# Transformer block with two feed-forward layers: sums of down weight blocks on VectorE, another order of the seven block products, norms of the first rows given row by row

## Chip, cores and metric

The kernel runs on one core of one Trainium2 chip. The metric is device time in microseconds of one execution. A profiled execution gives a trace; its span runs from the first instruction to the last. In the profile PE is TensorE (PEld its weight loads), DVE is VectorE, ACT is ScalarE, POOL is GpSimd, and SP is the engine whose queue issues the DMAs.

## What is computed

One encoder layer on x of 1024 tokens by 1024 features, float32:

```python
f = swiglu(rmsnorm(x, ffn1_pre_g), ffn1_w_gate, ffn1_w_up, ffn1_w_down)   # silu(h @ Wg) * (h @ Wu) @ Wd
x = x + 0.5 * rmsnorm(f, ffn1_post_g)
h = rmsnorm(x, mix_pre_g);  qkv = h @ w_qkv
x = x + rmsnorm(concat(attention_a(qkv), attention_b(qkv)) @ w_out, mix_post_g)
f = swiglu(rmsnorm(x, ffn2_pre_g), ffn2_w_gate, ffn2_w_up, ffn2_w_down)
x = x + 0.5 * rmsnorm(f, ffn2_post_g)
```

The hidden width of the feed-forwards is 2816 = 22 x 128. The change touches the down projection h @ Wd of both feed-forwards and the norm behind it; attention is as it was.

## The kernel before, in words

Products of float32 are made of three passes: each operand is split into a high part, rounded by ScalarE (L118), and a low part, the rest (L119, on VectorE or GpSimd); high by high, high by low and low by high are added in PSUM.

The down projection is done as a seven-product block scheme. Tokens are halved (y rows T = 0 to 3 and 4 to 7), output columns are halved (0 to 511, 512 to 1023), and the hidden rows are taken in 11 pairs of two blocks of 128. For pair j the weight blocks b11, b12 (rows of the first block) and b21, b22 (of the second) are 128x512 each. Seven products k = 0 to 6 of a left factor (a sum of blocks of the hidden activations, kept in DRAM as hd) and a right factor take the place of eight. The right factors are, in turn: 0: b11; 1: b21; 3: d = b22 - b12; 2: s = b11 + d; 4: b21 - s; 5: b22 - s; 6: b22. `prepare_down` (L247 to L269) makes them in place: on GpSimd d in b12 (L261) and s in b11 (L262) at product 0, b21 - s in b12 (L264) and b22 - s in b11 (L265) at product 3.

The pairs are worked in two groups, of 5 and of 6 pairs, and each group goes through the seven products in the order DOWN = 0, 2, 3, 4, 5, 1, 6; within a product over the pairs. One item is one product of one pair: `down` (L343) issues 12 matmuls, three passes into each of four PSUM banks (i = 0 to 3). Products 0 and 1 add up in four banks of the pool psd, the others in the banks pa to pd of the pools psg0 and psg1; a product in `first` starts its banks new, the others go on adding. When the last pair of a product is done its four banks are read: product 0 into U by ScalarE (L369), product 2 is added to U (L371), the others go to the quarters of y with or without U (L378, L380, L382). In the second group U is added to three quarters of y by twelve delayed adds (L374), kept in the list `late`.

`run` (L441) goes through the items. Before each, `feed` (L201) prepares tiles of split factors until five (WBUFS) are ahead of TensorE; an item of the down projection uses two, one of each factor. Then one delayed job is taken from `late`: besides the twelve adds these are the last sums of left factors, each with its store to hd (L336, L337). After some items of the last two products of the second group (n - at = 0 for the first item of product 1, 6 for the first of product 6) `run` calls jobs: `begin1` loads gains and residuals; `post1((4, 5))` norms two finished rows of y at once, `rms_pair` (L96) giving both factors and `post_scale` (L526) doing both rows (L534, L535) with one store each; `mix1` (L628) is the norm ahead of the attention projection; `early1` and `early2` do squares and the gain product (L552, on GpSimd) of the first 512 columns of rows 0 to 3; `first_q` splits the first projection weight (L582, L583); `to_actT` (L111) turns a row on TensorE (L107) through psd. The last item does products of the last two pairs bank by bank, and `row1` or `row2` finishes each of rows 0 to 3.

Each engine works off its instructions in the order of its queue. The framework sets this order from the source order and the dependences, so that a queue can take a later instruction first (a store of the last pair's left factor, L330, is issued at 455.89 us, before the loop reaches the end of that pair). A load that takes a buffer over waits in the SP queue for its last reader. Of each weight block there are 6 buffers. b11 of the first five pairs is loaded when the gate and up products end (L430), in the space that the raw gate weights leave; b22, b12 and b21 at product 0; those of the second group one block per product, at products 4, 5, 1 and 6 of the first group (L269).

Of the kernel before, what the change touches and what calls it, by code (L numbers as in the profile page):

```python
# [20 lines left out]
D = 1024  # L21
# [15 lines left out]
def tile_macaron_block(ctx, tc, x, f1_pre, f1_post, f1_g, f1_u, f1_d, mix_pre, mix_post, w_qkv,  # L37
# [83 lines left out]
    class Ffn:  # L121
# [10 lines left out]
        PAIRS = NF // 2  # L132
        DOWN = (0, 2, 3, 4, 5, 1, 6)
        GROUPS = (tuple(range(PAIRS // 2)), tuple(range(PAIRS // 2, PAIRS)))
# [5 lines left out]
        def __init__(self, wg, wu, wd, tag, far):  # L140
            self.wg, self.wu, self.wd, self.tag, self.far = wg[0], wu[0], wd[0], tag, far
            self.near = "left" if far == "right" else "right"
            self.W, self.RAW, self.H, self.P, self.B, self.Q = {}, {}, {}, {}, {}, {}
            self.A, self.S = {}, {}
            self.items = [("G", i, p) for i in range(1, NF) for p in (self.ORDER if i < NF - 1 else self.LAST)]
            downs = [("D", k, j) for g in self.GROUPS for k in self.DOWN for j in g]
            self.items += downs
            self.tiles = []
            for it in self.items:
                self.tiles += [it] if it[0] == "G" else [it + (z,) for z in range(2)]  # L150
            self.wanted = [d[1:] for d in downs]
            self.hd = {}
            for key in self.wanted:
                self.hd[key] = dram.tile([128, 512], F32, name=f"hd{tag}" + "_".join(str(z) for z in key))
            self.made = self.used = 0
            self.dw = {}
            self.late = []

# [88 lines left out]
        def prepare_down(self, k, j, part):  # L247

            sub, add, tt = OP.subtract, OP.add, POOL.tensor_tensor
            if part == 0:  # L250
                self.load_left(1)
                self.split_w((j, k, 0), self.A.pop((k, j)), DVE)
                return
            n = len(self.GROUPS[0])
            if k == 0 and j < n:
                for b in ("b22", "b12", "b21"):
                    self.load_block(j, b)
            b11, b12, b21, b22 = [self.B[j, name] for name in self.BLOCKS]
            self.split_w((j, k, 1), (b11, b21, b11, b12, b12, b11, b22)[k], DVE)
            if k == 0:  # L260
                tt(b12, b22, b12, op=sub)  # L261
                tt(b11, b12, b11, op=add)  # L262
            elif k == 3:
                tt(b12, b21, b11, op=sub)  # L264
                tt(b11, b22, b11, op=sub)  # L265
            elif k in (1, 4, 5, 6) and j < n:
                for after in ((n,) if j == 0 else ()) + (j + n + 1,):
                    if after < self.PAIRS:
                        self.load_block(after, {4: "b12", 5: "b11", 1: "b21", 6: "b22"}[k])  # L269

# [72 lines left out]
        def down(self, k, js, y, ps, psd, row=None):  # L343
            g = js[0] in self.GROUPS[1]
            start, end = js[0] == self.GROUPS[g][0], js[-1] == self.GROUPS[g][-1]
            first = k in (0, 2, 3, 5)
            U, add, tt = self.U, OP.add, DVE.tensor_tensor
            Q = self.Q.setdefault(k < 2, {})
            for i in range(4):
                if first and start:  # L350
                    if k == 0:
                        Q[i] = psd.tile([128, 512], F32, name="pd")
                    else:
                        Q[i] = ps[i // 2].tile([128, 4, 128], F32, name="p" + "abcd"[i]).rearrange("p t f -> p (t f)")
# [9 lines left out]

                def yv(T, d):
                    return y[:, T, 512 * d:512 * d + 512]

                if k == 0:
                    ACT.activation(U[i], p, AF.Copy)  # L369
                elif k == 2:  # L370
                    tt(U[i], U[i], p, op=add)  # L371
                    if g:
                        for v in (yv(i + 4, 1), yv(i + 4, 0), yv(i, 1)):
                            self.late.append(lambda v=v, i=i: tt(v, v, U[i], op=add))  # L374
                else:
                    v = {1: yv(i, 0), 3: yv(i + 4, 1), 4: yv(i + 4, 0), 5: yv(i + 4, 1), 6: yv(i, 1)}[k]
                    if g or k == 5:
                        tt(v, v, p, op=add)  # L378
                    elif k == 1:
                        ACT.activation(v, p, AF.Copy)  # L380
                    else:
                        tt(v, U[i], p, op=add)  # L382
                if row:
# [7 lines left out]
        def gate_up(self, i, prod, ps, y, psd):  # L391
# [32 lines left out]
            if i == NF - 1 and n == 3:  # L424
                self.close_tx(3)
                self.raw.release()
                self.load_left(self.AHEAD)
                self.open_blocks(("b11", "b12"), self.far)
                self.open_blocks(("b22", "b21"), self.near)
                for j in self.GROUPS[0]:  # L430
                    self.load_block(j, "b11")
            if n == 6 and i % 2 == 1:
# [8 lines left out]
        def run(self, ps, y, psd, jobs, row):  # L441
# [4 lines left out]
            for n, it in enumerate(self.items):  # L446
                if n == at:
                    self.add_late(len(self.late))
                    for name in ("b12", "b11"):
                        self.dw[name].release()  # L450
                self.feed()
                self.add_late(1)
                if it[0] == "G":
# [69 lines left out]
    def junk(T):  # L523
        return actT[:, HI, :, T]
# [20 lines left out]
    def post_early(T, g):  # L545

        if T % 2 == 0:
# [3 lines left out]
                       accum_out=SS[T // 2][:, 0, T % 2:T % 2 + 1])  # L551
        POOL.tensor_tensor(yh, yh, g[:, 0:512], op=OP.mult)  # L552

# [67 lines left out]

    def post1(Ts):
        r = rms_pair([y[:, T, :] for T in Ts], [junk(T - 4) for T in Ts])
        post_scale(Ts, r, E1["g"], [E1["xr", T] for T in Ts], lambda T: x1d[T])
        for T in TS[TS.index(Ts[0]) + 2:TS.index(Ts[0]) + 4]:
            E1["xr", T] = load_res(E1["pre"], lambda T: xrow(xv, T), T, 2)

# [9 lines left out]
    def early1():  # L637
        for T in range(4):
            post_early(T, E1["g"])

    def row1(i):
        post_late(i)
        if i % 2 == 1:
# [4 lines left out]

    f1.run((psg0, psg1), y, psd,
           {0: [begin1, lambda: post1((4, 5))], 3: [lambda: mix1((4, 5))], 4: [lambda: post1((6, 7))],  # L650
            5: [early1], 6: [lambda: mix1((6, 7))], 7: [first_q], 8: [lambda: to_actT(4, y[:, 4, :], psd)],
            9: [lambda: to_actT(5, y[:, 5, :], psd)]}, row1)
    psg1.release()
# [7 lines left out]

    def turn1(T):
        to_actT(T, y[:, T, :], psd)

    mix1((0, 1))
# [431 lines left out]

    def post2(Ts):
        r = rms_pair([y[:, T, :] for T in Ts], [junk(T - 4) for T in Ts])
        post_scale(Ts, r, E2["g"], [E2["xr", T] for T in Ts], lambda T: xrow(ov, T))  # L1100

# [7 lines left out]

    f2.run((psg0, psg1), y, psd, {0: [begin2, lambda: post2((4, 5))], 4: [lambda: post2((6, 7))], 5: [early2]}, row2)  # L1110
    psg1.release()
# [71 lines left out]
```

## Time and profile before

| | us |
|---|---|
| median of 3 runs | 2070.18 |
| lowest and highest | 2069.85, 2072.19 |
| the profiled execution | 2066.44 |
| its span | 2064.7 |
| TensorE busy in the span | 1986.9 |
| VectorE, ScalarE, GpSimd busy | 1353.2, 1030.1, 995.4 |
| mean granted clock of TensorE | 0.992 |

The down projection of the first feed-forward lies from 473.84 to 717.04 us, that of the second from 1817.28 to 2052.00. A matmul's busy time overlaps with the next one's, so stretches are compared by their length from first start to next start. Idle time in a row of the timeline stands in brackets, with the instruction that ended it.

### The profile page before, as it was taken

The page shows a single profiled execution, that of the slowest core. Times are in us where ns is not written, and L with a number is a line of the kernel's source. Part 1 is how long each engine was busy: PE and PEld are TensorE (multiplying, and loading weights), DVE is VectorE, ACT ScalarE, POOL GpSimd, SP SyncE. Part 2 cuts the span into 40 slices and gives each one's busy share as a digit, 9 for nine tenths or more (in the row PEclk, how much of TensorE's full clock was granted, in tenths as well). Part 3 has the DMA queues.
Part 4 walks back from the last instruction along what each step waited for, and adds up shares of the span by engine and source line. Part 5 has one row for each costly group of instructions (what it writes and reads, how often), then busy time and mean ns, then how long its engine had stood idle before and what let it go on. Part 6 is the DMA issues. An engine that isn't in the chain of part 4 may idle for free. (4 is left out here: it accounts for less than half of the span.)

```text
span 2064.7 us, 30519 instructions
## 1 busy us (share of the span) xinstructions
PE 1986.9 (96%) x10704; PEld 1676.6 (81%) x10704; DVE 1353.2 (66%) x2323; ACT 1030.1 (50%) x1977; POOL 995.4 (48%) x864
## 2 busy tenths in 40 slices
PE   7999999999998899999999999999999999999986
PEld 6777777777776799998999998887777777777775
DVE  7555454558667948766988887365555545586678
ACT  5433333334443844546999998234333333344434
POOL 4566656655142102124777887315566566651421
PEclk9999999999999999999999999999999999999998
DMA  4233332327533462232040752322323324275333
GB/s 148 72 103 98 107 102 82 123 92 260 174 113 93 165 182 89 76 92 60 1 138 18 201 137 82 104 74 72 102 87 118 103 77 128 84 268 174 112 104 152
DMA packets 212440, 235.62 MB, mean 114 GB/s; under 512 B 22208, under 2 KB 148160, under 8 KB 212160
## 3 DMA queue, kind: packets, MB, share of 16 engines
q1 hardware_dynamic: 212288, 233.69, 36.3%
q8 instruction: 84, 1.38, 0.3%
q14 instruction: 68, 0.56, 0.1%
HBM read 166.01 MB, written 67.63 MB: 113 GB/s over the span
## 5 line engine op out<-in xcount | busy, mean ns | idle before, releaser
L119 POOL TENSOR_TENSOR wgu<-rawgu,wgu 128x512 fp32r<-128x512 f32 x216 | 313.4, 1460 | 362.1 <-ACT wgu L118 334.7
L118 ACT ACTIVATE wgu<-rawgu 128x512 fp32r<-128x512 f32 x302 | 181.7, 628 | 378.0 <-POOL rawgu L227 189.8
L286 PE MATMUL pa<-actT,wgu 128*128 128x512 f32 (+1 forms) x1080 | 270.5, 398 | 8.9 <-ACT U L405 8.1
L286 PEld LDWEIGHTS pa<-actT,wgu 128*128 128x128 f32 x1080 | 198.6, 191 | 65.3 <-ACT U L405 20.3
L359 PE MATMUL pd<-wgu 128*128 128x512 f32 x858 | 218.6, 396 | 7.3 <-DVE wgu L119 7.3
L118 ACT ACTIVATE wgu<-b 128x512 fp32r<-128x512 f32 x154 | 97.1, 630 | 247.0 <-PE pd L359 143.4
L595 PE MATMUL pq<-wq,actT 128*128 128x256 f32 x1728 | 214.8, 281 | 0.0
L595 PEld LDWEIGHTS pq<-wq,actT 128*128 128x128 f32 x1728 | 206.2, 188 | 0.2
L119 DVE TENSOR_TENSOR wgu<-b,wgu 128x512 fp32r<-128x512 f32 x154 | 128.2, 833 | 109.8 <-ACT wgu L118 109.4
L359 PEld LDWEIGHTS pd<-wgu 128*128 128x128 f32 x858 | 164.0, 192 | 44.5 <-DVE wgu L119 9.4
L821 POOL TENSOR_SCALAR P<-P,il 128x1024 f32<-128x1024 f32 (+1 forms) x128 | 130.4, 1019 | 67.0 <-DVE il L820 62.4
L439 DVE TENSOR_TENSOR h<-h,C 64x512 f32<-64x512 f32 x42 | 49.6, 1181 | 159.5 <-ACT h L438 159.4
L922 DVE TENSOR_TENSOR PT<-pt,PT 128x512 fp32r<-128x512 f32 (+1 forms) x256 | 146.3, 613 | 2.1 <-ACT PT L921 2.0
L286 PE MATMUL pc<-actT,wgu 128*128 128x512 f32 x552 | 136.5, 396 | 0.0
L286 PE MATMUL pd<-actT,wgu 128*128 128x512 f32 x552 | 136.0, 395 | 0.0
L921 ACT ACTIVATE PT<-pt 128x512 fp32r<-128x512 f32 (+1 forms) x256 | 125.2, 544 | 13.6 <-PE pt L918 10.1
L119 DVE TENSOR_TENSOR wgu<-h,wgu 128x512 fp32r<-128x512 f32 x154 | 126.2, 820 | 1.8 <-ACT wgu L118 1.8
L918 PE MATMUL pt<-identr,P 128*128 128x128 f32 x896 | 124.9, 274 | 1.7 <-ACT vst L756 1.1
L286 PEld LDWEIGHTS pd<-actT,wgu 128*128 128x128 f32 x552 | 103.4, 187 | 25.3
L286 PEld LDWEIGHTS pc<-actT,wgu 128*128 128x128 f32 x552 | 103.4, 188 | 25.3 <-DVE actT L109 0.4
L359 PE MATMUL pa<-wgu 128*128 128x512 f32 x330 | 100.8, 404 | 23.6 <-DVE wgu L119 14.0
L286 PE MATMUL pb<-tx,wgu 128*128 128x512 f32 x504 | 122.8, 392 | 0.0
(189 smaller groups left out, 4052.8 us busy)
## 6 DMA issues: line engine op xcount, KB each, us to landing
hd<-h SPq DMA_DIRECT2D x154, 256.0 KB, 2.8
h<-hd SPq DMA_DIRECT2D x154, 256.0 KB, 2.8
rawgu<-in_ffn_w_gate_dram SPq DMA_DIRECT2D x88, 256.0 KB, 3.0
rawgu<-in_ffn_w_up_dram SPq DMA_DIRECT2D x88, 256.0 KB, 3.5
b<-in_ffn_w_down_dram SPq DMA_DIRECT2D x88, 256.0 KB, 3.2
bkT<-kd SPq DMA_DIRECT2D x32, 320.0 KB, 8.0
rawq<-in_w_qkv_dram SPq DMA_DIRECT2D x16, 512.0 KB, 4.7
bV<-vd SPq DMA_DIRECT2D x8, 640.0 KB, 4.6
```

The lines of the kernel that those rows point to most:

```text
L118: ACT.activation(hi, raw, AF.Copy)
L119: return eng.tensor_tensor(lo, raw, f32(hi), op=OP.subtract).ins
L286: PE.matmul(p[:, c0:c1, :], w[:, a, k, :], self.rhs(name, b, k)[:, c0:c1, :], start=(first and n == 0), stop=(n == 11), skip_group_check=True)
L359: PE.matmul(p, A[:, a, 128 * i:128 * i + 128], B[:, b, :], start=(first and start and j == js[0] and n == 0), stop=(end and j == js[-1] an ...
L439: DVE.tensor_tensor(dst, s[64:128], c[64:128], op=OP.mult)
L595: PE.matmul(p, actT[:, a, k, T, :], WQ[j][:, b, k, :], start=(n == 0), stop=(n == 23))
L821: POOL.tensor_scalar(P[:, 0:w], P[:, 0:w], il, 1.0, op0=OP.mult, op1=OP.mult)
L918: PE.transpose(out=p[:, j, :], in_=col(P, b0 + j), identity=ident)
L921: ACT.activation(hv, p[:, 0:n, :], AF.Copy)
L922: DVE.tensor_tensor(lv, p[:, 0:n, :], f32(hv), op=OP.subtract)
```

## The change

The block sums and the gain product of `post_early` move from GpSimd to VectorE. The first group takes the products in the order 1, 0, 2, 3, 6, 4, 5; the second keeps its order. In the first group products 0, 3 and 4 use the banks of psd and 1, 2, 6 and 5 those of psg0 and psg1, and y00 and y01 get one product more by an add of their own. d of the second group's pairs is made in the first group's product 5; b11 = b22 - s moves to product 4. b21 is loaded first, and b22, b12 and b11 at product 1. The delayed adds of the second group are left out of product 3, taken at every second item of product 4 and at every item of product 5; those of one quarter (`late2`) follow in product 1. The jobs on rows 4 to 7 are given row by row, and `mix1((6, 7))` goes behind the loop.

```diff
         PAIRS = NF // 2
-        DOWN = (0, 2, 3, 4, 5, 1, 6)
+        DOWN = ((1, 0, 2, 3, 6, 4, 5), (0, 2, 3, 4, 5, 1, 6))
         GROUPS = (tuple(range(PAIRS // 2)), tuple(range(PAIRS // 2, PAIRS)))
...
             self.items = [("G", i, p) for i in range(1, NF) for p in (self.ORDER if i < NF - 1 else self.LAST)]
-            downs = [("D", k, j) for g in self.GROUPS for k in self.DOWN for j in g]
+            downs = [("D", k, j) for n, g in enumerate(self.GROUPS) for k in self.DOWN[n] for j in g]
             self.items += downs
...
             self.dw = {}
-            self.late = []
+            self.late, self.late2 = [], []
...
-            sub, add, tt = OP.subtract, OP.add, POOL.tensor_tensor
+            sub, add, tt = OP.subtract, OP.add, DVE.tensor_tensor
             if part == 0:
...
             n = len(self.GROUPS[0])
-            if k == 0 and j < n:
-                for b in ("b22", "b12", "b21"):
+            after = [z for z in ((n,) if j == 0 else ()) + (j + n + 1,) if j < n and z < self.PAIRS]
+            if k == 1 and j < n:
+                for b in ("b22", "b12", "b11"):
                     self.load_block(j, b)
...
             self.split_w((j, k, 1), (b11, b21, b11, b12, b12, b11, b22)[k], DVE)
-            if k == 0:
-                tt(b12, b22, b12, op=sub)
+
+            def diff(j):
+                tt(self.B[j, "b12"], self.B[j, "b22"], self.B[j, "b12"], op=sub)
+
+            if k == 1 and j < n:
+                diff(j)
+            elif k == 0:
                 tt(b11, b12, b11, op=add)
...
                 tt(b12, b21, b11, op=sub)
+            elif k == 4:
                 tt(b11, b22, b11, op=sub)
-            elif k in (1, 4, 5, 6) and j < n:
-                for after in ((n,) if j == 0 else ()) + (j + n + 1,):
-                    if after < self.PAIRS:
-                        self.load_block(after, {4: "b12", 5: "b11", 1: "b21", 6: "b22"}[k])
+            for z in after:
+                for b in {3: ("b21",), 4: ("b12", "b22"), 5: ("b11",)}.get(k, ()):
+                    self.load_block(z, b)
+                if k == 5:
+                    diff(z)
...
             start, end = js[0] == self.GROUPS[g][0], js[-1] == self.GROUPS[g][-1]
-            first = k in (0, 2, 3, 5)
+            first = k in ((0, 2, 3, 5) if g else (0, 1, 2, 3, 5, 6))
+            side = k < 2 if g else k in (0, 3, 4)
             U, add, tt = self.U, OP.add, DVE.tensor_tensor
-            Q = self.Q.setdefault(k < 2, {})
+            Q = self.Q.setdefault(side, {})
             for i in range(4):
                 if first and start:
-                    if k == 0:
+                    if side:
                         Q[i] = psd.tile([128, 512], F32, name="pd")
...
-                def yv(T, d):
-                    return y[:, T, 512 * d:512 * d + 512]
-
+                y00, y01, y10, y11 = [y[:, T, 512 * d:512 * d + 512] for T in (i, i + 4) for d in range(2)]
                 if k == 0:
                     ACT.activation(U[i], p, AF.Copy)
+                    if not g:
+                        tt(y00, y00, p, op=add)
                 elif k == 2:
...
                     if g:
-                        for v in (yv(i + 4, 1), yv(i + 4, 0), yv(i, 1)):
-                            self.late.append(lambda v=v, i=i: tt(v, v, U[i], op=add))
+                        self.late += [lambda v=v, i=i: tt(v, v, U[i], op=add) for v in (y11, y10)]
+                        self.late2.append(lambda v=y01, i=i: tt(v, v, U[i], op=add))
+                elif g:
+                    v = {1: y00, 3: y11, 4: y10, 5: y11, 6: y01}[k]
+                    tt(v, v, p, op=add)
+                elif k == 1:
+                    ACT.activation(y00, p, AF.Copy)
+                elif k == 5:
+                    tt(y11, y11, p, op=add)
+                    tt(y01, y01, p, op=add)
                 else:
-                    v = {1: yv(i, 0), 3: yv(i + 4, 1), 4: yv(i + 4, 0), 5: yv(i + 4, 1), 6: yv(i, 1)}[k]
-                    if g or k == 5:
-                        tt(v, v, p, op=add)
-                    elif k == 1:
-                        ACT.activation(v, p, AF.Copy)
-                    else:
-                        tt(v, U[i], p, op=add)
+                    tt({3: y11, 4: y10, 6: y01}[k], U[i], p, op=add)
                 if row:
...
                 for j in self.GROUPS[0]:
-                    self.load_block(j, "b11")
+                    self.load_block(j, "b21")
             if n == 6 and i % 2 == 1:
...
                 if n == at:
-                    self.add_late(len(self.late))
+                    self.late += self.late2
+                    self.add_late(len(self.late) - len(self.late2))
                     for name in ("b12", "b11"):
...
                 self.feed()
-                self.add_late(1)
+                if n < at - 18 or n >= at - 6 or n >= at - 12 and n % 2 == 0:
+                    self.add_late(1)
                 if it[0] == "G":
...
                        accum_out=SS[T // 2][:, 0, T % 2:T % 2 + 1])
-        POOL.tensor_tensor(yh, yh, g[:, 0:512], op=OP.mult)
+        DVE.tensor_tensor(yh, yh, g[:, 0:512], op=OP.mult)
...
-    def post1(Ts):
-        r = rms_pair([y[:, T, :] for T in Ts], [junk(T - 4) for T in Ts])
-        post_scale(Ts, r, E1["g"], [E1["xr", T] for T in Ts], lambda T: x1d[T])
-        for T in TS[TS.index(Ts[0]) + 2:TS.index(Ts[0]) + 4]:
-            E1["xr", T] = load_res(E1["pre"], lambda T: xrow(xv, T), T, 2)
+    def stat1(Ts):
+        for T, z in zip(Ts, rms_pair([y[:, T, :] for T in Ts], [junk(T - 4) for T in Ts])):
+            E1["r", T] = z
+
+    def post1(T):
+        post_scale((T,), [E1["r", T]], E1["g"], [E1["xr", T]], lambda T: x1d[T])
+        T = TS[TS.index(T) + 2]
+        E1["xr", T] = load_res(E1["pre"], lambda T: xrow(xv, T), T, 2)
...
             post_early(T, E1["g"])
+
+    def turn1(T):
+        to_actT(T, y[:, T, :], psd)
...
     f1.run((psg0, psg1), y, psd,
-           {0: [begin1, lambda: post1((4, 5))], 3: [lambda: mix1((4, 5))], 4: [lambda: post1((6, 7))],
-            5: [early1], 6: [lambda: mix1((6, 7))], 7: [first_q], 8: [lambda: to_actT(4, y[:, 4, :], psd)],
-            9: [lambda: to_actT(5, y[:, 5, :], psd)]}, row1)
+           {0: [begin1, lambda: stat1((4, 5)), lambda: post1(4)], 1: [lambda: post1(5)], 3: [lambda: mix1((4, 5))],
+            5: [early1], 6: [first_q], 7: [lambda: stat1((6, 7)), lambda: post1(6)], 8: [lambda: post1(7)],
+            9: [lambda: turn1(4), lambda: turn1(5)]}, row1)
     psg1.release()
...
-    def turn1(T):
-        to_actT(T, y[:, T, :], psd)
-
+    mix1((6, 7))
     mix1((0, 1))
...
-    def post2(Ts):
-        r = rms_pair([y[:, T, :] for T in Ts], [junk(T - 4) for T in Ts])
-        post_scale(Ts, r, E2["g"], [E2["xr", T] for T in Ts], lambda T: xrow(ov, T))
+    def stat2(Ts):
+        for T, z in zip(Ts, rms_pair([y[:, T, :] for T in Ts], [junk(T - 4) for T in Ts])):
+            E2["r", T] = z
+
+    def post2(T):
+        post_scale((T,), [E2["r", T]], E2["g"], [E2["xr", T]], lambda T: xrow(ov, T))
...
-    f2.run((psg0, psg1), y, psd, {0: [begin2, lambda: post2((4, 5))], 4: [lambda: post2((6, 7))], 5: [early2]}, row2)
+    f2.run((psg0, psg1), y, psd, {
+        0: [begin2, lambda: stat2((4, 5))], 1: [lambda: post2(4)], 2: [lambda: post2(5)], 3: [lambda: stat2((6, 7))],
+        4: [lambda: post2(6)], 5: [early2], 6: [lambda: post2(7)]}, row2)
     psg1.release()
...
     psg0.release()
```

## Rows read from the trace of the kernel before

**Rows 1.** The page, part 1: busy time, share of the span, instructions.

```profile
PE 1986.9 (96%) x10704; PEld 1676.6 (81%) x10704; DVE 1353.2 (66%) x2323; ACT 1030.1 (50%) x1977; POOL 995.4 (48%) x864
```

**Rows 2.** Windows of down projection 1: stretch, length, busy us (instructions), clock, DMA share, GB/s.

```profile
473.84:487.50 13.66, 13.66 (x61) 11.18 (x60) 12.37 (x13) 7.18 (x13) 7.24 (x5) 1.00 0.79 272
487.50:503.33 15.83, 14.54 (x62) 10.87 (x60) 12.67 (x15) 6.40 (x12) 6.74 (x5) 1.00 0.93 315
503.33:520.61 17.28, 14.17 (x60) 11.11 (x61) 16.46 (x15) 6.92 (x12) 16.34 (x11) 1.00 0.40 123
520.61:609.84 89.23, 89.19 (x385) 73.09 (x385) 52.13 (x81) 39.67 (x70) 18.91 (x13) 0.98 0.49 151
609.84:636.51 26.67, 17.91 (x72) 13.12 (x73) 26.67 (x27) 8.06 (x14) 18.17 (x12) 1.00 0.20 60
636.51:670.45 33.94, 33.92 (x142) 27.59 (x142) 20.48 (x33) 12.69 (x22) 0.02 (x1) 0.95 0.39 112
670.45:717.04 46.59, 38.71 (x165) 31.19 (x163) 42.12 (x76) 36.51 (x71) 7.11 (x5) 0.93 0.53 182
```

**Rows 3.** Windows of down projection 2, same columns.

```profile
1831.09:1846.47 15.38, 14.36 (x61) 10.95 (x60) 12.21 (x14) 6.39 (x12) 6.70 (x5) 1.00 0.96 335
1846.47:1863.78 17.31, 14.16 (x61) 11.11 (x61) 16.55 (x15) 6.92 (x12) 16.37 (x11) 1.00 0.37 111
1863.78:1952.72 88.94, 87.92 (x385) 71.84 (x385) 54.61 (x81) 39.69 (x70) 18.67 (x13) 1.00 0.48 151
1952.72:1979.40 26.68, 20.94 (x72) 15.21 (x73) 26.68 (x27) 7.72 (x14) 18.17 (x12) 0.87 0.20 59
...
2011.75:2052.00 40.25, 36.37 (x148) 28.17 (x146) 35.57 (x61) 22.24 (x46) 7.56 (x5) 0.96 0.40 156
```

**Rows 4.** Timeline of PE: start us, length us, what, and idle before it.

```profile
520.61 1.38 PE L359 MATMUL pa<-wgu 128*128 128x512 f32 x3 [2.97 <-DVE y L382]
...
695.91 1.47 PE L107 MATMUL pd<-identr,y 128*128 128x128 f32 x12
702.35 1.12 PE L107 MATMUL pd<-identr,y 128*128 128x128 f32 x4 [4.96 <-DVE y L378]
```

**Rows 5.** Timeline of DVE, same columns.

```profile
609.01 0.68 DVE L371 TENSOR_TENSOR U<-U,pa 128x512 f32<-128x512 f32 x1
609.61 0.68 DVE L371 TENSOR_TENSOR U<-U,pb 128x512 f32<-128x512 f32 x1
...
621.90 3.47 DVE L374 TENSOR_TENSOR y<-y,U 128x512 f32<-128x512 f32 x2
...
639.29 0.68 DVE L374 TENSOR_TENSOR y<-y,C 128x512 f32<-128x512 f32 x1
...
677.87 2.47 DVE L534 SCALAR_TENSOR_TENSOR y<-y,rs_y,gpost 128x1024 f32<-128x1024 f32 x2
680.26 2.35 DVE L535 TENSOR_TENSOR y<-y,xr 128x1024 f32<-128x1024 f32 x2
...
695.94 3.48 DVE L534 SCALAR_TENSOR_TENSOR y<-y,rs_y,gpost 128x1024 f32<-128x1024 f32 x2
```

**Rows 6.** Timeline of POOL, same columns.

```profile
621.46 1.68 POOL L264 TENSOR_TENSOR b<-b,b 128x512 f32<-128x512 f32 x1 [1.83 <-DVE wgu L119]
...
2038.73 7.14 POOL L552 TENSOR_TENSOR y<-y,gpost 128x512 f32<-128x512 f32 x4 [26.55 <-ACT actT L550]
```

**Rows 7.** Weight blocks b, 440 to 520 us: issues (ns), what idle time ended on, landing.

```profile
L237 SPq DMA_DIRECT2D b<-in_ffn_w_down_dram x25: 328/430/472, 458.6 to 518.2; - x25
...
  DMA b<-in_ffn_w_down_dram: 18.0, 4
...
DMA to landing us min/median/max: 2.5/4.3/5.8
```

**Rows 8.** The same, 1795 to 1850 us.

```profile
  DMA b<-in_ffn_w_down_dram: 13.9, 4
```

**Rows 9.** Timeline of ACT, same columns as PE's.

```profile
708.35 2.19 ACT L631 ACTIVATE y<-y,rs_y 128x1024 f32<-128x1024 f32 x2 [0.98 <-DVE rs_y L88]
```

## The prediction, made before the run

> **What bounds the kernel now.** The page comes first: TensorE is busy for 96% of the span, VectorE for 66%, GpSimd for 48% [rows 1]. Over the whole span only TensorE is near its limit, so a change of VectorE and GpSimd work can pay only in stretches where TensorE waits. The windows come next, one per stage of the two down projections, cut where TensorE starts a product. One item (one product of one pair) is twelve matmuls. The first window is five items in 13.66 us, 2.73 us each, with hardly a wait; everything is measured against that [rows 2, 3].
>
> By this measure the first feed-forward loses, stage by stage: 15.83 - 5 x 2.73 = 2.2 us in the second product of the first group; 17.28 - 13.7 = 3.6 in the third; 89.23 - 32 x 2.73 = 1.8 over the next 32 items (385 matmuls), where the granted clock is 0.98; 26.67 - 6 x 2.73 = 10.3 in the third product of the second group; 33.94 - 12 x 2.73 = 1.1 after it, clock 0.95; and in the last stage 46.59 - 12 x 2.73 - 16 transposes of 0.12 (twelve took 1.47 [rows 4]) = 11.8. Together 30.8 us. The second feed-forward loses 1.7, 3.6, 1.5, 10.3 and 40.25 - 32.8 = 7.5, together 24.6 us [rows 3]. So at most about 55 us are to be had here.
>
> The timelines say who is late. Before the fourth product of the first group TensorE sits idle for 2.97 us until VectorE has read the PSUM bank that this product goes on adding to [rows 4]. In the 10.3 us stage VectorE is busy for 26.67 of 26.67 us with 27 instructions [rows 2]. An add of 128x512 alone takes 0.68 us, and in a row they follow each other by 0.60 (609.01 to 609.61); two that run beside a GpSimd sum take 3.47, some 1.74 each, and the same line is back at 0.68 at 639.29, when GpSimd has finished [rows 5, 6]. 27 x 0.60 is 16.2, so about 10.5 us of that stage is VectorE held up by GpSimd, as much as TensorE loses.
>
> **The change, part by part.**
>
> *The sums.* 88 GpSimd instructions of about 1.7 us [rows 6] become 88 VectorE adds of 0.60, 53 us in all, 26 per feed-forward. Per item VectorE then has two splits and one sum, 1.8 us, and 2.4 where a kept sum or a delayed add comes along, below the 2.73 us of TensorE. The hold-up goes with the GpSimd sums. The twelve delayed adds of U also leave the third product for the two after it, one per two items and then one per item, and the last four go to product 1. The 10.3 us stage should then cost what its matmuls cost, and a change-over of product at its end that costs between nothing and one add, 0.68; I take 0.2. Gain 10.1 in each, and the 1.1 of low clock that follows in the first: 21.3 us. The second product of the first group gives back up to 2.2 + 1.7 = 3.9 of the same kind.
>
> The Trainium skill speaks against this: "Perfetto Trace Analysis", section Optimizing Scalar/DVE Operations, lets a saturated VectorE hand work to GpSimd, though it adds that the shared read port may spoil it. This is the opposite move, onto a VectorE that is full in that stage; taken alone the rule makes it a loss (third rival). The trace agrees with the rule's proviso: 1.74 against 0.68.
>
> *The order of the first group.* In 1, 0, 2, 3, 6, 4, 5 the products alternate between the two sets of PSUM banks, so each set has a whole product (13.7 us) to be read. The 2.97 us wait goes, in both feed-forwards: 2 x (3.6 - 0.2) = 6.8, and with it most of the low clock behind it in the first, 1.5 of the 1.8. It adds eight VectorE reads of PSUM per feed-forward (y00 once, y01 once more, four each), 4.8 us in a stage where VectorE is busy 52.13 of 89.23 us [rows 2]: nothing, as long as that cover is there.
>
> *What the new order makes VectorE wait for.* b12 = b22 - b12 now stands right behind the split of the first product, and b22, b12 and b11 are only then asked for. Until now GpSimd took this wait, 18.0 us in four waits in the first feed-forward, 13.9 in the second, and nothing stood behind it [rows 7, 8]. Behind VectorE's stand the splits for TensorE. Lower bound: nothing, for TensorE has five tiles, 6.8 us, in hand and the queue may place the difference later. Upper bound: all 31.9 us on VectorE, 3.2 per difference. With 2.4 of its own work, 5.6 per item against 2.73 is 2.9 late, five times, less the 6.8 in hand: 7.6 per feed-forward, 15 in both. Most waits are shorter than the lead, so I take 6. The b21 loads, now the first, go into the space of the turned tiles and so wait for their last product; the SP queue stands behind them, but product 1 starts later: part of the same 6. Other loads move from one per product to one, two and one in products 3, 4 and 5, at 0.43 us of SP each [rows 7], with one to two products until they are used: nothing. The differences for the second group are made in the first group's last product, when b12 and b22 were asked for a product earlier: nothing. Eight adds at that product's end, 4.8 us, are within the 6.8 in hand.
>
> *The norms.* Rows 4 and 5 are normed one after the other, rows 6 and 7 three items later in the first feed-forward, and after product 1's banks are read. Today a pair is 2.47 + 2.35 us in one piece on VectorE, and once 3.48 + 2.35 in front of the read for which TensorE's transposes waited 4.96 us [rows 4, 5]. But these stages are nearly full: VectorE works 42.12 of 46.59 and 35.57 of 40.25 us [rows 2, 3]. The change adds 4 first-half gain products and 4 late adds, 8 x 0.60 = 4.8, and takes off the hold-up by the four GpSimd products: about 1.0 each by the 3.48 against the 2.47, 4 in the first; in the second, where they stand in one piece of 7.14 us [rows 6] and VectorE is idle for more of the time, I take 3. 42.9 and 37.4 us of VectorE remain, of which about one may lie behind TensorE's last product. Gain 46.6 - 41.9 = 4.7 and 40.25 - 36.4 = 3.8. Bounds: none, and all of 11.8 + 7.5.
>
> *mix1 of rows 6 and 7* goes behind the loop: squares, root and two scalings (2.19 us [rows 9]) before their transposes. The projections of rows 4 and 5 stand in front; from nothing to 5 us, taken as 2. The final tail of rows 0 to 3 is as before: 0.
>
> *Sum:* 21.3 + 3.9 + 6.8 + 1.5 + 8.5 - 6 - 2 = 34.0 us. The profiled execution took 2066.44 us (span 2064.7 and 1.7 around it), 3.7 below the median of the runs, 2070.18. Against the median: 2036.
>
> **The rivals.** First, the last stages keep their length: VectorE is the bound there, and what the row-by-row norms save goes to the added products. For it: 42 of 46.6 us busy. Against: the 4.96 us wait has one cause, and that is moved. 34.0 - 8.5 = 25.5: 2045.
>
> Second, slower: the difference in product 1 parks VectorE. The place is the first five items of each down projection. If SP lets the three loads go only when the split before is done, each difference waits 3 x 0.43 + 4.3 (median landing) = 5.6 us, or 7.1 with the longest, 5.8 [rows 7]. An item then takes 2.4 + 5.6 = 8.0, 5.3 too long, five times, less 6.8: 19.5 per feed-forward, 39 in both, against a gain of 40 without this term: 2069. With the longest landing it is 27 each, 54: 2084. It decides from 4.0 us lost per difference. For it: GpSimd did wait here. Against: only 3.2 each on average, and part of that before the down projection began.
>
> Third, slower too, the rule above as a mechanism: VectorE is simply full, and each sum and product put on it lengthens its full stages: 12 x 0.60 in the stage of 26.67 and 4.8 in the last, 12 per feed-forward: 2094. Against: the slow adds coincide with GpSimd's, and the same line takes 0.68 without them.
>
> That the new order doesn't spread the load would show as the 2.97 us wait at another change of product; it is within the first rival's time.
>
> **How the numbers follow.** Forecast 0.60, last stages unchanged 0.22, parked VectorE 0.13 (of which 0.03 still faster, 0.05 level, 0.05 slower), full VectorE 0.05. A measurement of this kernel can tell about 0.2%, 4 us. Faster: 0.60 + 0.22 + 0.03 = 0.85; level 0.05; slower 0.10. Low end: both unknown costs at nothing (8) and most of the rest of the last stages (8 of 10.8): 2020. High end: waits at 15, mix1 at 5 and no gain in the last stages make 2056; with a little of the second rival, 2060. That leaves out about 2 in 10.
>
> **What would show it.** Right: no VectorE add of 128x512 over 1 us in the down projections, a stage of six items in 16.4 to 17 us where it took 26.7, no wait at the fourth product, GpSimd idle there. Wrong: VectorE idle behind a weight-block DMA in the first five items of each down projection, with TensorE waiting for splits there; or last stages still of 46 and 40 us; or a gap at the first projections, waiting for row 6.

## The result and the profile after

The changed kernel takes 2039.33 us (median of 4 runs, 2038.66 to 2042.67) against 2070.01 (2067.09 to 2072.19): ratio 0.9856, 95% interval 0.9839 to 0.9873. The forecast was 2036, with a range of 2020 to 2060. The profiled execution took 2038.71 us with a span of 2036.9.

The page of the changed kernel, part 1, answers to [rows 1]:

```profile
PE 1976.9 (97%) x10704; PEld 1675.1 (82%) x10704; DVE 1351.0 (66%) x2435; ACT 1030.5 (51%) x1977; POOL 840.7 (41%) x768
```

GpSimd gives up 96 instructions and 155 us. VectorE takes 112 more and is busy for 2 us less: what it took on, 88 sums, 16 reads of PSUM and 8 gain products, cost it no more than the hold-up that it lost.

The windows of the changed kernel, cut at the same kind of places, first those of down projection 1, its last line the stretch behind it (columns as in [rows 2]):

```profile
471.64:499.44 27.80, 27.58 (x122) 22.39 (x120) 23.71 (x39) 15.88 (x29) 0.00 (x0) 1.00 0.93 320
499.44:526.69 27.25, 27.25 (x121) 22.45 (x120) 22.95 (x39) 12.13 (x22) 0.00 (x0) 1.00 0.52 170
526.69:554.32 27.63, 27.52 (x122) 22.45 (x120) 20.78 (x35) 11.53 (x20) 0.00 (x0) 1.00 0.59 191
554.32:586.22 31.90, 30.21 (x134) 24.70 (x132) 24.64 (x41) 14.06 (x25) 0.00 (x0) 1.00 0.43 132
586.22:603.32 17.10, 16.48 (x73) 13.36 (x72) 9.11 (x15) 8.11 (x16) 0.00 (x0) 1.00 0.35 97
603.32:619.94 16.62, 16.60 (x72) 13.44 (x73) 16.37 (x28) 6.34 (x12) 0.00 (x0) 1.00 0.32 92
619.94:652.31 32.37, 32.35 (x141) 26.47 (x142) 26.24 (x43) 13.84 (x24) 0.00 (x0) 1.00 0.38 115
652.31:694.70 42.39, 37.35 (x164) 30.25 (x163) 37.90 (x71) 31.34 (x62) 1.06 (x1) 0.96 0.52 174
694.70:740.00 45.30, 40.63 (x312) 39.79 (x311) 28.70 (x76) 30.95 (x67) 0.00 (x0) 0.89 0.55 167
```

Two of down projection 2, the third product of its second group and its last stage:

```profile
1933.67:1950.29 16.62, 16.60 (x73) 13.44 (x73) 16.37 (x28) 6.34 (x12) 0.00 (x0) 1.00 0.30 89
...
1982.65:2024.20 41.55, 37.07 (x148) 28.69 (x146) 34.91 (x63) 22.46 (x46) 0.44 (x1) 0.92 0.39 152
```

The third product of the second group, which took 26.67 and 26.68 us [rows 2, 3], takes 16.62 in both: six items at 2.73 and a change-over. VectorE is still busy for 16.37 of it, now with 28 instructions at 0.60 instead of 27 at almost 1. The first twenty items take 55.1 us, 54.6 being the measure. The last stages are what is left: 42.39 us in the first down projection (46.59 before), 41.55 in the second, where it was 40.25.

In all, down projection 1 goes from 243.2 us to 223.1 and down projection 2 from 234.7 to 222.1: 32.7 us less. Between the two lie 1107.4 us instead of 1100.2, 7.2 more. The tail behind the last matmul is 12.7 us in both. The rest of the span's 27.8 is in front: the first down projection began at 473.84 us before and at 471.64 here. In the ten profiled executions of this study it began between 471.0 and 473.8, also in two of one and the same kernel 0.5 apart, so these 2.2 us are not put down to the change.

The timeline of PE in the changed kernel shows the waits that are left, or new (the idle time before each in brackets):

```profile
573.39 6.87 PE L368 MATMUL pd<-wgu 128*128 128x512 f32 x29 [1.69 <-DVE wgu L119]
...
665.14 9.18 PE L368 MATMUL pd<-wgu 128*128 128x512 f32 x32 [2.92 <-DVE wgu L119]
...
690.03 0.96 PE L368 MATMUL pa<-wgu 128*128 128x512 f32 x3 [2.12 <-DVE wgu L119]
...
704.61 3.68 PE L107 MATMUL pd<-identr,y 128*128 128x128 f32 x16 [4.08 <-ACT y L647]
...
2008.75 1.22 PE L368 MATMUL pa<-wgu 128*128 128x512 f32 x2 [3.84 <-DVE wgu L119]
```

The first comes at the start of the second group, once in each down projection. The timeline of DVE says why for all but the one at 704.61: pieces of other work stand in one row in front of the splits (L119) that TensorE waits for. (The wait at 704.61 is for ScalarE; the run with the norm inside the loop takes it up.)

```profile
566.67 0.68 DVE L119 TENSOR_TENSOR wgu<-h,wgu 128x512 fp32r<-128x512 f32 x1
...
567.88 0.68 DVE L390 TENSOR_TENSOR y<-y,pa 128x512 f32<-128x512 f32 x1
...
572.06 0.68 DVE L391 TENSOR_TENSOR y<-y,pd 128x512 f32<-128x512 f32 x1
572.66 0.68 DVE L119 TENSOR_TENSOR wgu<-b,wgu 128x512 fp32r<-128x512 f32 x1
...
659.74 2.48 DVE L547 SCALAR_TENSOR_TENSOR y<-y,rs_y,gpost 128x1024 f32<-128x1024 f32 x2
662.13 2.35 DVE L548 TENSOR_TENSOR y<-y,xr 128x1024 f32<-128x1024 f32 x2
664.40 0.68 DVE L119 TENSOR_TENSOR wgu<-b,wgu 128x512 fp32r<-128x512 f32 x1
...
684.63 2.47 DVE L547 SCALAR_TENSOR_TENSOR y<-y,rs_y,gpost 128x1024 f32<-128x1024 f32 x2
687.02 2.35 DVE L548 TENSOR_TENSOR y<-y,xr 128x1024 f32<-128x1024 f32 x2
689.29 0.68 DVE L119 TENSOR_TENSOR wgu<-b,wgu 128x512 fp32r<-128x512 f32 x1
...
2003.69 1.88 DVE L386 TENSOR_TENSOR y<-y,pd 128x512 f32<-128x512 f32 x3
2005.49 2.61 DVE L565 TENSOR_TENSOR y<-y,gpost 128x512 f32<-128x512 f32 x4
2008.01 0.68 DVE L119 TENSOR_TENSOR wgu<-b,wgu 128x512 fp32r<-128x512 f32 x1
```

From 567.88 to 572.66 stand the eight reads of the four banks of product 5 (L390, L391). At 659.74 rows 4 and 5 are still normed together: the source gives them row by row, at items 0 and 1, and the queue has put them side by side again, scaling with scaling. At 684.63 it has done the same with rows 6 and 7, which the source gives at items 7 and 8. In the second down projection the rows do come one by one (from 1990.94). At 2005.49 the four gain products that came from GpSimd stand in one piece behind three reads of PSUM.

### The profile page after: what moved, and what is told of

It is laid out like the page before. It is cut to its first block, busy times and chain, and to the rows that moved or that the text cites. A ratio compares the mean times of both kernels' runs of the same rounds, so it can differ in the third digit from the quotient of the medians.

```text
span 2036.9 us, 30471 instructions
## 1 busy us (share of the span) xinstructions
PE 1976.9 (97%) x10704; PEld 1675.1 (82%) x10704; DVE 1351.0 (66%) x2435; ACT 1030.5 (51%) x1977; POOL 840.7 (41%) x768
## 4 chain that ended last, share of the span: by engine, by line
PE 70%; POOL 11%; ACT 6%; DVE 5%; issue 4%; DMA 3%; SPq 0%; DVEq 0%; ACTq 0%; POOLq 0%
PE pq L608 10%; PE pd L368 8%; PE pa L294 8%; PE pc L294 6%; PE pd L294 5%; PE pt L935 5%; POOL wgu L119 5%; PE pz L1073 4%; PE pb L294 3%; PE pa L368 3%; ACT wgu L118 3%; PE po L959 3%; PE pb L368 3%; PE pc L368 3%; PE sp L845 3%
## 5 line engine op out<-in xcount | busy, mean ns | idle before, releaser
L119 POOL TENSOR_TENSOR wgu<-rawgu,wgu 128x512 fp32r<-128x512 f32 x216 | 312.9, 1457 | 359.5 <-ACT wgu L118 333.4
L118 ACT ACTIVATE wgu<-rawgu 128x512 fp32r<-128x512 f32 x302 | 181.7, 628 | 377.6 <-POOL rawgu L227 189.6
L368 PE MATMUL pd<-wgu 128*128 128x512 f32 x948 | 236.3, 393 | 7.5 <-DVE wgu L119 6.9
L368 PEld LDWEIGHTS pd<-wgu 128*128 128x128 f32 x948 | 178.3, 189 | 49.2 <-DVE wgu L119 10.6
L118 ACT ACTIVATE wgu<-b 128x512 fp32r<-128x512 f32 x154 | 97.2, 631 | 218.9 <-PE pd L368 209.6
L119 DVE TENSOR_TENSOR wgu<-b,wgu 128x512 fp32r<-128x512 f32 x154 | 106.1, 689 | 76.5 <-ACT wgu L118 76.4
L294 PE MATMUL pc<-tx,wgu 128*128 128x512 f32 x504 | 122.4, 392 | 0.0
```

The source lines that it names most:

```text
L118: ACT.activation(hi, raw, AF.Copy)
L119: return eng.tensor_tensor(lo, raw, f32(hi), op=OP.subtract).ins
L294: PE.matmul(p[:, c0:c1, :], w[:, a, k, :], self.rhs(name, b, k)[:, c0:c1, :], start=(first and n == 0), stop=(n == 11), skip_group_check=True)
L368: PE.matmul(p, A[:, a, 128 * i:128 * i + 128], B[:, b, :], start=(first and start and j == js[0] and n == 0), stop=(end and j == js[-1] an ...
```

## The experiments

Each is compared with the kernel before, run on the same chip. The length of a down projection is read from the timeline of PE, from its first matmul to the end of its last.

| kernel | median us | ratio, 95% interval | down projections 1 + 2, us |
|---|---|---|---|
| changed kernel | 2039.33 | 0.9856 (0.9839 to 0.9873) | 223.2 + 222.2 |
| sums back on GpSimd | 2063.89 | 0.9987 (0.9971 to 1.0002) | 234.0 + 235.1 |
| sums alone | 2043.50 | 0.9895 (0.9879 to 0.9911) | 230.3 + 225.9 |
| jobs by pairs | 2040.91 | 0.9884 (0.9867 to 0.9900) | 225.8 + 228.1 |
| norm inside the loop | 2034.47 | 0.9849 (0.9835 to 0.9864) | 223.9 + 221.7 |
| changed kernel again | 2040.51 | 0.9874 (0.9855 to 0.9892) | 224.6 + 222.2 |
| old order | 2043.85 | 0.9887 (0.9871 to 0.9903) | 227.9 + 222.6 |
| gain products on GpSimd | 2034.14 | 0.9839 (0.9821 to 0.9858) | 225.0 + 221.1 |
| bursts spread | 2024.28 | 0.9796 (0.9780 to 0.9812) | 220.0 + 216.1 |

The kernel before was at 2066.28 beside the second to the fifth (243.4 + 234.7 in its profile), at 2066.64 beside the last four.

**Sums back on GpSimd**, order, jobs and delayed adds as changed.

```diff
-            sub, add, tt = OP.subtract, OP.add, DVE.tensor_tensor
+            sub, add, tt = OP.subtract, OP.add, POOL.tensor_tensor
```

> The changed kernel with the 88 block sums back on GpSimd; order, jobs and delayed adds stay as changed. Theory 1 (the hold-up of VectorE by GpSimd is what the move takes away): VectorE adds of 1.7 us beside GpSimd sums are back, some 1.1 us per sum, and where sums, splits and adds meet TensorE waits again; 2045 to 2058 us. Theory 2 (the new order and the spread of the sums do it, the engine hardly matters): VectorE has 2 splits and one hold-up per item, 2.3 us against 2.72, so the third product of the second group stays at 17 us; 2037 to 2043 us.

2063.89 us: of the whole gain 2 us are left, and the interval reaches past 1. Theory 1 holds, though the time lies outside its range too. The third product of the second group takes 23.7 us again (608.58 to 632.24 in the timeline of PE) where the changed kernel takes 16.62. Timeline of DVE in the third product of the second group, and of POOL beside it:

```profile
613.15 1.78 DVE L119 TENSOR_TENSOR wgu<-b,wgu 128x512 fp32r<-128x512 f32 x1
614.85 0.68 DVE L119 TENSOR_TENSOR wgu<-h,wgu 128x512 fp32r<-128x512 f32 x1
...
628.04 1.78 DVE L119 TENSOR_TENSOR wgu<-b,wgu 128x512 fp32r<-128x512 f32 x1
```

```profile
612.75 1.63 POOL L272 TENSOR_TENSOR b<-b,b 128x512 f32<-128x512 f32 x1
615.01 1.67 POOL L270 TENSOR_TENSOR b<-b,b 128x512 f32<-128x512 f32 x1 [0.63 <-DVE wgu L119]
...
627.53 1.74 POOL L270 TENSOR_TENSOR b<-b,b 128x512 f32<-128x512 f32 x1
```

The split that starts at 613.15, beside a sum, takes 1.78 us and ends 0.55 us after that sum, at 614.93; the one at 614.85, which starts between the sum's end at 614.38 and the next sum at 615.01, takes 0.68. GpSimd runs L270 and L272 in turn, although the source has put L272 a product later, and five of the delayed adds (L382, L383) still run in this stage; so this run alone doesn't try theory 2, because the spread in the source did not reach the queues. In the changed kernel VectorE also runs L270 and L272 in turn, and only one delayed add is left in the stage. The next run leaves the spread out altogether.

**Sums alone**: the kernel before, with the one line of `prepare_down` the other way round, POOL to DVE.

> The kernel before with its 88 block sums on VectorE and nothing else changed. Theory 1 (hold-up alone): the stage of 26.7 us falls to 17 in both down projections, 2045 to 2052 us. Theory 2 (spreading matters): the third product of the second group then holds 12 splits, 12 sums, 12 delayed adds and 4 reads of PSUM, 40 x 0.60 = 24 us of VectorE, and in the first group the wait before the fourth product stays near 3 us; 2057 to 2066 us.

2043.50 us, a little below theory 1's 2045 to 2052, but not quite for its reason. Windows and timeline of PE:

```profile
602.68:622.54 19.86, 17.06 (x73) 13.29 (x73) 19.86 (x34) 7.49 (x14) 0.00 (x0) 1.00 0.29 83
```

```profile
514.44 0.93 PE L359 MATMUL pa<-wgu 128*128 128x512 f32 x3 [0.63 <-DVE y L382]
...
622.54 0.93 PE L359 MATMUL pa<-wgu 128*128 128x512 f32 x3 [2.80 <-DVE y L378]
```

The third product falls from 26.67 to 19.86, not to 17: VectorE is full for all of it, with 34 instructions at 0.58, and TensorE waits 2.80 us for the reads behind them. That part is theory 2's, and it is what the delayed adds had to be moved away for. And the wait of 2.97 us before the fourth product of the first group [rows 4] is 0.63 us here, in the old order with the old banks (0.62 in the second down projection).

**Old order**: the changed kernel with 0, 2, 3, 4, 5, 1, 6 in both groups, and the banks, the loads, the reads of PSUM and the places of the sums that belong to it; the sums stay on VectorE, delayed adds and jobs as changed. The cut shows the order and the banks only.

```diff
-        DOWN = ((1, 0, 2, 3, 6, 4, 5), (0, 2, 3, 4, 5, 1, 6))
+        DOWN = (0, 2, 3, 4, 5, 1, 6)
...
-            first = k in ((0, 2, 3, 5) if g else (0, 1, 2, 3, 5, 6))
-            side = k < 2 if g else k in (0, 3, 4)
+            first = k in (0, 2, 3, 5)
```

> The changed kernel with both groups in the order 0, 2, 3, 4, 5, 1, 6 as before; the sums on VectorE, the delayed adds and the jobs as changed. The prediction's step (the new order takes away the 2.97 us wait at the fourth product and the low clock behind it, 8.3 us in all): 8 us slower than the changed kernel. Reading of the run with the sums alone, where that wait fell to 0.63 us in the old order: it was VectorE's hold-up and not the bank, so 0 to 3 us slower.

2043.85 against 2040.51 on the same chip. The intervals overlap; the down projections are 3.7 us longer by the profiles, 3.3 of it in the first. So the order, with all that belongs to it, is worth at most some 3 us, which the medians can't tell from nothing, and not 8. The wait at the fourth product is again 0.62:

```profile
518.00 0.93 PE L359 MATMUL pa<-wgu 128*128 128x512 f32 x3 [0.62 <-DVE y L383]
```

**Jobs by pairs**: the changed kernel with the job lists of before (`mix1((6, 7))` inside the loop with them).

```diff
-           {0: [begin1, lambda: stat1((4, 5)), lambda: post1(4)], 1: [lambda: post1(5)], 3: [lambda: mix1((4, 5))],
+           {0: [begin1, lambda: stat1((4, 5)), lambda: both1((4, 5))], 3: [lambda: mix1((4, 5))],
+            4: [lambda: stat1((6, 7)), lambda: both1((6, 7))],
...
-    mix1((6, 7))
     mix1((0, 1))
```

> The changed kernel with the job lists of the kernel before: pairs of rows normed together at items 0 and 4, the norm ahead of the projections for rows 6 and 7 inside the loop. The prediction's step (row by row gains 8.5 in the last stages, the moved norm costs 2): 2045 to 2048 us. Reading of the changed kernel's trace (the queue still does rows 4 and 5 together in the first feed-forward, the moved norm costs 4 us of wait and as much in clock): the job part is worth nothing or less, 2033 to 2041 us.

2040.91, beside 2039.33 and 2040.51 of the changed kernel on other chips: level, as the trace had said. The down projections are longer by 8.5 us (223.2 to 225.8, 222.2 to 228.1), and the stretch between them gives 7.5 of it back. So two parts of the change cancel here: norms row by row are worth something in the down projections, and the norm behind the loop costs as much behind the first. The next run, on the same chip, has the first part without the second: 2034.47, so jobs row by row are worth 6.4 us there (that norm also stands at item 9 instead of 6).

**Norm inside the loop**: the changed kernel with only this norm moved back.

```diff
-            9: [lambda: turn1(4), lambda: turn1(5)]}, row1)
+            9: [lambda: mix1((6, 7)), lambda: turn1(4), lambda: turn1(5)]}, row1)
...
-    mix1((6, 7))
     mix1((0, 1))
```

> The changed kernel with the norm of rows 6 and 7 ahead of the projections called at item 9 inside the loop instead of behind it. If its place costs what the trace shows, the 4.08 us wait before the transposes of rows 6 and 7 goes, and with it the low clock behind it: 2030 to 2035 us. Rival (ScalarE and VectorE are full there, the same work only waits elsewhere): 2038 to 2042 us.

2034.47 us. The down projections keep their length; the gain is behind them. Timeline of PE and window, to be held against 704.61 and 694.70:740.00 above:

```profile
698.93 0.98 PE L107 MATMUL pd<-identr,y 128*128 128x128 f32 x7 [1.10 <-ACT y L647]
699.67 3.08 PE L608 MATMUL pq<-wq,actT 128*128 128x256 f32 x24
702.58 0.27 PE L107 MATMUL pd<-identr,y 128*128 128x128 f32 x1
```

```profile
696.70:742.00 45.30, 43.80 (x373) 43.26 (x372) 29.84 (x74) 29.45 (x66) 0.00 (x0) 1.00 0.62 186
```

In 45.30 us TensorE issues 373 matmuls instead of 312, at a granted clock of 1.00 instead of 0.89.

**Changed kernel again**, unchanged, as a measure. 

> The changed kernel once more, as a measure for the others of this group on the same chip: 2034 to 2041 us.

 It came to 2040.51.

**Gain products on GpSimd**: the kernel with the norm inside the loop, L565 back on POOL.

> The kernel with the norm of rows 6 and 7 inside the loop (2034 us in its run), with the four gain products of rows 0 to 3 back on GpSimd. If these four products in one piece of 2.6 us are what makes TensorE wait 3.8 us in the last stage of the second feed-forward: that wait falls to 1 us or less, 2 to 4 us faster than it. If the hold-up of VectorE by GpSimd counts for more: level to 4 us slower than it, with adds of 1.7 us in the last stages.

2034.14 against 2034.47: level, which is the edge of the second reading; the first, 2 to 4 us faster, fails. The one long wait (3.84 us in the changed kernel, 4.12 in the kernel with the norm inside the loop) becomes three (timeline of PE, and of DVE and POOL below it):

```profile
2005.89 0.74 PE L368 MATMUL pa<-wgu 128*128 128x512 f32 x2 [1.32 <-DVE wgu L119]
...
2010.40 0.74 PE L368 MATMUL pa<-wgu 128*128 128x512 f32 x2 [1.68 <-DVE wgu L119]
...
2013.84 0.74 PE L368 MATMUL pa<-wgu 128*128 128x512 f32 x2 [0.87 <-DVE wgu L119]
```

```profile
2006.36 2.32 DVE L547 SCALAR_TENSOR_TENSOR y<-y,rs_y,gpost 128x1024 f32<-128x1024 f32 x1
2008.60 1.75 DVE L119 TENSOR_TENSOR wgu<-b,wgu 128x512 fp32r<-128x512 f32 x1
...
2005.60 5.89 POOL L565 TENSOR_TENSOR y<-y,gpost 128x512 f32<-128x512 f32 x3 [0.99 <-ACT actT L563]
```

On VectorE the four products are a burst, on GpSimd a hold-up; the waits come to much the same, 4.1 and 3.9 us.

**Bursts spread**: the kernel with the norm inside the loop, and three bursts taken apart.

```diff
-                    tt(y01, y01, p, op=add)
+                    self.late.append(lambda v=y01, p=p: tt(v, v, p, op=add))
...
-           {0: [begin1, lambda: stat1((4, 5)), lambda: post1(4)], 1: [lambda: post1(5)], 3: [lambda: mix1((4, 5))],
-            5: [early1], 6: [first_q], 7: [lambda: stat1((6, 7)), lambda: post1(6)], 8: [lambda: post1(7)],
+           {0: [begin1, lambda: stat1((4, 5))], 1: [lambda: post1(4)], 2: [lambda: post1(5)], 3: [lambda: mix1((4, 5))],
+            5: [lambda: post_early(0, E1["g"])], 6: [first_q, lambda: post_early(1, E1["g"])],
+            7: [lambda: stat1((6, 7)), lambda: post1(6), lambda: post_early(2, E1["g"])],
+            8: [lambda: post1(7), lambda: post_early(3, E1["g"])],
...
-        4: [lambda: post2(6)], 5: [early2], 6: [lambda: post2(7)]}, row2)
+        4: [lambda: post2(6)], 5: [lambda: post_early(0, E2["g"])], 6: [lambda: post2(7)],
+        7: [lambda: post_early(1, E2["g"])], 8: [lambda: post_early(2, E2["g"])], 9: [lambda: post_early(3, E2["g"])]}, row2)
```

> The kernel with the norm of rows 6 and 7 inside the loop, and three bursts of VectorE spread: rows 4 and 5 of the first feed-forward at items 1 and 2 instead of 0 and 1, the gain products of rows 0 to 3 one per item, and the second add of product 5 in the first group as a delayed add. If bursts are what makes TensorE wait there (1.69 us at the start of the second group, 2.92 and 3.8 us in the last stages): these waits fall under 1 us each and the time to 2022 to 2029 us. If VectorE is simply full in the last stages, the waits move to other items there: 2030 to 2035 us.

2024.28 us, 16 below the changed kernel on the same chip and 42 below the kernel before. Of the 16 some 6 belong to the norm inside the loop, which this kernel has too; against the two runs with that norm (2034.14, 2034.47) the spread is worth 10. VectorE does the same work; the wait of 1.69 us is gone in both places, and what stays in the last stages is, by the timeline of PE:

```profile
684.56 0.96 PE L368 MATMUL pa<-wgu 128*128 128x512 f32 x3 [2.89 <-DVE wgu L119]
...
1994.90 0.73 PE L368 MATMUL pa<-wgu 128*128 128x512 f32 x2 [1.96 <-DVE wgu L119]
```

Not all waits fell under 1 us, as had been expected, but VectorE was not full either. In front of the wait at 684.56 rows 6 and 7 are still normed together (from 679.16), a burst that this run left as it was. How the gain divides over the three bursts was not tried one by one.

## Why the prediction was right, and where its steps were not

**The sums: right, and larger than put.** The 10.3 us stage came out at 16.62 where 16.4 to 17 was said, twice, and the second product's 2.2 and 1.7 came with it. Run alone the move is worth 23 us of the median; taken out of the changed kernel it takes all but 2 us along. That it is GpSimd's presence that makes a VectorE instruction 1.78 us long was argued from coincidence; the run with the sums put back shows it, in the same line and stage. One reading was wrong without harm: the adds at 609.01 and 609.61, called alone, ran beside a GpSimd sum (timeline of POOL in the kernel before):

```profile
608.62 1.63 POOL L264 TENSOR_TENSOR b<-b,b 128x512 f32<-128x512 f32 x1 [17.43 <-issue]
```

They kept to 0.68 all the same. They read one input from PSUM, and the instructions that are held up have both in SBUF; the last section counts them. The price of 0.60 stands, for the changed kernel's sums take it.

The rule of the Trainium skill ("Perfetto Trace Analysis", Optimizing Scalar/DVE Operations) that a saturated VectorE may hand work to GpSimd does not hold here: the opposite move gains, which its own proviso, that the two share an SBUF read port, leaves room for. What the runs show is the hold-up, 0.68 against 1.78; that it is the port, none of them shows.

**The order of the first group: right effect, wrong cause.** The step put 8.3 us down to the banks. The wait of 2.97 us did go, but with the sums on VectorE it goes in the old order too (0.63 and 0.62): VectorE was late at the bank because it was held up. What the order adds is some 3 us. So the term belonged to the sums, and the total stood.

**VectorE behind the loads of product 1: sized 6, cost next to nothing.** VectorE did wait there, but 2.2 us in three waits in the first down projection, and 2.5 in three in the second: some 0.5 us per difference, where the second rival needed 4.0. TensorE's five tiles covered that: it shows no wait of 0.5 us in those items, and the first twenty lost 0.5 to 0.7 us in all. The view is that of the weight blocks from 455 to 500 us in the changed kernel; of its four waits for DMA, 5.1 us, the first, 2.9, is ScalarE's (L118), before the down projection begins:

```profile
  DMA b<-in_ffn_w_down_dram: 5.1, 4
...
  ACT wgu L118: 2.9, 1
  DVE b L263: 2.2, 3
...
DMA to landing us min/median/max: 2.5/4.4/6.3
```

The second rival's fall did not come. The eight adds at the end of product 5, which had been set at nothing because 4.8 is less than 6.8, cost 1.69 us each time: the cover was counted as if it were full when the burst began. When the last split before it ended, at 567.35, TensorE had 4.4 us of work in hand and not 6.8: it ran out at 571.70.

**The last stages: one right, one wrong.** The first came to 42.39, 41.9 having been said. In the second the step took a total of work (36.4 us) for the length of the stage; it became 41.55, longer than before. Work that fits in the sum may still stand in the wrong place: the four products in one piece, behind three reads of PSUM, went with a wait of 3.84 us and a clock of 0.92 over the stage. Moving them back to GpSimd gained nothing; taking the bursts apart did. And "row by row" was taken from the source; in the first down projection the queue did not follow it, for either pair. The idea was sound all the same: with the norm inside the loop, row by row is worth 6.4 us against pairs.

**The norm behind the loop: sized 2, bounded by 5, cost about 7.** The stretch between the projections is 7.2 us longer than before, and the run with the norm inside the loop is 6.0 faster in the median (2034.47 against 2040.51, on two chips whose times for the kernel before are 0.4 apart). The wait of 4.08 us was inside the bound; the low clock behind it was left out. In the 45.30 us of the two windows TensorE issues 61 matmuls fewer (312 against 373); at 0.12 us each (with the norm inside the loop 24 run from 699.67 to the next one at 702.58, at full clock) that is 7.4 us. Of these 3.2 are more idle time (45.30 less 40.63 and less 43.80), the other 4 go with the clock of 0.89.

So errors of both signs met. Costs were put 6 too high for the loads, and too low by some 5 for the norm, 5 for the second feed-forward's last stage and 3 for the eight adds; the order's 8.3, mostly the sums' own, left the total as it was. That the forecast came within 3.3 us is in part luck: some 13 us too little stood against 6 too much, and half of the gap that was left closed because the sum, worked out from the profiled execution at 2066.44, was taken off a median 3.7 higher. From one profiled execution to the other the gain is 27.7 us, where the sum said 34.0; by the medians it is 30.7.

## What to carry to other kernels

Before work is moved between GpSimd and VectorE, read one VectorE instruction with both inputs in SBUF alone and beside a GpSimd one: here 0.68 and 1.78 us, so that a GpSimd sum cost VectorE more than doing it itself. Then look at the longest row of other work in front of what TensorE waits for, rather than at the busy share: the same work, spread, gave another 10 us. And price a wait of TensorE with the clock that follows it, read from the rows behind it.

## What the runs showed of the hardware that had not been expected

The hold-up has a plain form. In the two down projections of the kernel before and of the run with the sums back on GpSimd, 129 VectorE instructions on 128x512 with both inputs in SBUF start while a GpSimd instruction runs; all but one of them end 0.53 to 0.65 us after that GpSimd instruction, however early they start in it. A lone one lasts 0.66 to 0.69. The 58 that read one input from PSUM and start beside GpSimd take 0.67 to 0.69, as if it were not there.

The granted clock after a wait of 4.08 us: in the 45.30 us that hold it, it is 0.89 on average (levels 1.2 and 2.4 GHz), where with a wait of 1.10 in the same place it stays at 1.00. The waits of 2.92 and 2.12 us in the stage before went with 0.96 over 42.39 us. By the count of matmuls above, the low clock cost about 4 us beside 3.2 us of added idle time. In windows of about 3 us the clock is 0.50 from the end of the wait at 704.60 to 711.00, 0.57 to 714.00 and 1.00 behind that; the 16 transposes at 704.61 take 0.23 us each, where twelve took 1.47 [rows 4]. The length of the wait alone does not give the price. Behind the 4.96 us of the kernel before [rows 4] it is 0.52 for 3 us and then 1.00. Behind a wait of 2.92 in the last stage it is 0.61 over 3 us in the changed kernel (665.14) and 1.00 in the run with the sums back on GpSimd (679.02). Behind 1.69 us it stayed at 1.00 in both places.
